# Weights' lower parts by ScalarE and an accumulating transfer, in one hybrid decoder layer in float32 on one core

## Chip, core and metric

One NeuronCore of a Trainium2 chip runs the whole layer as one program. The metric is the device time of one execution in microseconds (us). Engines: TensorE (PE), VectorE (DVE), ScalarE (ACT), GpSimd (POOL) and SyncE (SP), which here issues the transfers.

## What is computed

The input is x, 512 positions by 1024 channels in float32. In brief:

```python
proj = x @ w_in    # q, k, v of mixer A, q, k, v of mixer B, indexer q, k and weights, branch gates
# A: sparse attention, 12 heads of 64. Indexer scores of 8 heads choose 128 causal keys per query.
# B: dilated window attention, 12 heads in three groups, joined by their softmax denominators.
y = (sigmoid(gA) * (oA @ w_branch_a) + sigmoid(gB) * (oB @ w_branch_b)) @ w_out
x = LN(alpha * x + y)
x = LN(alpha * x + (silu(x @ w_ffn_gate) * (x @ w_ffn_up)) @ w_ffn_down)
```

All products are wanted to float32's accuracy.

## The kernel before

**Products of three.** TensorE multiplies in the type float32r, which keeps fewer bits. So each operand is split into an upper part hi, the value rounded to float32r, and a lower part lo, the value minus hi. A product is hi times hi, plus hi times lo, plus lo times hi: three matmuls of 128 x 128 weights with up to 512 columns.

**Units.** The weights lie in memory as units of 128 x 1024 (512 KB). `load_unit` (L354) takes one: a transfer from SP's queue into a buffer raw, a copy by ScalarE into whi (L363), and a subtraction raw minus whi into wlo (`sub`, L381) by an engine that the caller names. raw, whi and wlo have four buffers each. In the projections the callers name "POOL" (two subtractions of 128 x 512 on GpSimd) or, for the gates, "ANY" (GpSimd or VectorE). The first four units are loaded in four pieces together with x and are subtracted on VectorE or "ANY". From the branch products on (`load_unit("DVE")`, `halves`) VectorE subtracts.

**Tasks.** ORDER (L53) is a string of names that are carried out in that order. i0 to i3 project the indexer's queries, K its keys and weights, I0 to I3 are its scores, each T is four steps of the search for the 128 best keys. a0 to a11 project mixer A's queries and keys, W0 to W2 its values, H0 to H5 are pairs of its heads. d0 to d3, e0 to e7 and v project mixer B's queries, keys and values, B0 to B3 are its scores (`scores` L631, `pair_scores` L623), X the exchange of its softmax statistics, M0 to M3 its outputs. G0 to G15 are the gates. A projection of queries or keys does not come in the shape that the scores need: its rows are brought into place by moves, transfers from SBUF to SBUF that SP issues (`move`, and `put_s`; all SP transfers have line L347).

**The keys' chain.** `index_keys` takes three units (K), copies the keys (L696), turns them on VectorE (L706, L709, L710), has TensorE transpose them (L715), and splits the result (L718, L719). Only then the scores of I can start.

**The exchange.** `exchange` writes the statistics z1 and z23 to memory (d) and reads them back in the other order (z1r, z23n). `b_factors` (L867 to L876) makes factors of them, with which L891 (VectorE) and L892 (ScalarE) scale the probabilities; TensorE then transposes those (L787, in `b_mix`).

**What sets the order.** `Plan` records all operations with a cost in us and a lag, and `Plan.order` lays them out: whenever an engine is free it takes the ready operation that was recorded first. Costs and lags are the kernel's own numbers. The result is written out as each engine's instruction stream, and the engines keep to it: an engine that waits for one instruction does none of those behind it. In the plan GpSimd's operations and VectorE's "shared" ones exclude each other (TURNS).

Of the kernel before, what the change touches and what calls it, by code (L numbers as in the profile page):

```python
# [9 lines left out]
FT = mybir.dt.float32  # L10
# [39 lines left out]

ORDER = ("G10 i0 G12 G6 G2 e0 i1 i2 K e1 I1 d0 i3 I2 I3 G7 G1 d1 e4 I0 W0 d2 e2 B0 T T T T W2 e3 a8 B1 d3 T v G3 T "  # L53
         "e5 a0 T T e6 B2 T e7 B3 X W1 a1 G9 M1 a9 M0 a2 T G5 M3 M2 a3 a4 T a10 T T H1 G14 H0 a5 G8 a6 H4 H2 G15 "
         "a11 a7 H5 G13 H3 G11 G4 G0").split()

H = (slice(0, 64), slice(64, 128))
SWAP = [x ^ 8 for x in range(32)]
# [42 lines left out]
class Plan:  # L101
# [2 lines left out]

    LAT = {"PE": 0.2, "DVE": 0.16, "ACT": 0.17, "POOL": 0.12, "SP": 0.05}
    TO_PE = 0.22
    TURNS = {"DVE": "POOL", "POOL": "DVE"}
    SAME = {"PE": 0.0, "DVE": 0.13, "ACT": 0.155, "POOL": 0.1, "SP": 0.0}  # L110

    def __init__(self):
        self.ops, self.tags, self.groups, self.pools = [], {}, {}, {}
# [192 lines left out]
def layer(ctx, tc, xT, xN, pos, wp, bg, ln, cst, out):  # L306
# [2 lines left out]
    V, A, G = nc.vector, nc.scalar, nc.gpsimd  # L309

    pool = lambda name, bufs, **k: ctx.enter_context(tc.tile_pool(name=name, bufs=bufs, **k))
    NS = 82
    P.group("s", NS, pool("s", NS), "s")
    P.group("raw", 4, pool("raw", 4), "raw")
    P.group("whi", 4, pool("whi", 4), "whi")
# [37 lines left out]
    def load_unit(lo_eng, pieces=1):  # L353

        u = unit[0]
        unit[0] += 1
        raw, hi, lo = P.buf("raw", FT, (128, 1024)), P.buf("whi", FR, (128, 1024)), P.buf("wlo", FR, (128, 1024))
        n = 1024 // pieces

        def piece(i):  # L360
            c = slice(i * n, (i + 1) * n)
            dma(raw, lambda: raw[:, c], lambda: wp[u * 128:(u + 1) * 128, c], 512 * n, key=i)
            P.op("ACT", ac(n, 1), lambda e: A.activation(hi[:, c], raw[:, c], AF.Copy), [(raw, i)], [(hi, i)])  # L363
            m = n if lo_eng == "DVE" else min(n, 512)
            for j in range(n // m):
                x = slice(i * n + j * m, i * n + j * m + m)
                sub(lo_eng, m, lambda x=x: lo[:, x], lambda x=x: raw[:, x], lambda x=x: hi[:, x].bitcast(FT),
                    [(raw, i), (hi, i)], [(lo, (i * n + j * m) * KO // 1024)])
        if pieces == 1:
            piece(0)  # L370
        return hi, lo, pieces, piece
# [46 lines left out]
    def next_unit(lo_eng):  # L418
        return first_units.pop(0) if first_units else load_unit(lo_eng)
# [168 lines left out]

    def sides(name, j, puts, regroup=False, t0=0):

        p = project(next_unit("POOL"), t0=t0)
        if j == 0:
            turned[name] = rotated_parts(p, regroup, t0)
            return
        parts = plain_parts(p, regroup, t0)
        for s, put in enumerate(puts):
            for unit_, row, n, first in plain_rows(s):
                if unit_ == j - 1:
                    if first == 0:
                        put(turned[name], ROT * s, ROT, 0)  # L600
                    put(parts, row, n, ROT + first)
# [58 lines left out]

    def value_chunk():
        res = []
        natural([next_unit("POOL") for _ in range(2)], 4, 256, lambda b, p: res.append(value_tile(p)))
        return res

    def strided_values():


        ps = [P.buf("pv") for _ in range(NB)]
        for u in range(4):  # L670
            hi, lo = next_unit("POOL")[:2]
            for k in range(2):
                for b, p in enumerate(ps):
                    def f(e, hi=hi, lo=lo, k=k, ko=2 * u + k, b=b, p=p):
                        t = lambda x: nat(x.tile)[:, :, b]
                        w = slice(k * 512, k * 512 + 512)
                        nc.tensor.matmul(p.tile, t(xhi[ko]), hi[:, w], start=ko == 0, stop=False)
                        nc.tensor.matmul(p.tile, t(xlo[ko]), hi[:, w], start=False, stop=False)
                        nc.tensor.matmul(p.tile, t(xhi[ko]), lo[:, w], start=False, stop=ko == KO - 1)
                    P.op("PE", 3 * mm(512), f, [hi, lo, xhi[2 * u + k], xlo[2 * u + k]], [p])  # L680
        store["V0"], store["V1"] = [], []
        for p in ps:
            for i in range(2):
                store[f"V{i}"].append(value_tile(p, 256 * i))
# [4 lines left out]
    def index_keys():  # L689

        store["VB"] = []
        wi = fixed("wi", (128, NB, 8))
        kn = P.buf("rt", FT, (128, NB, 2, 64))

        def use(b, p):
            P.op("ACT", ac(128), lambda e: A.activation(  # L696
                kn[:, b], p[:, None, 256:320].to_broadcast([128, 2, 64]), AF.Copy), [p], [(kn, b), (p, 1)])
            store["VB"].append(value_tile(p))
            P.op("DVE", 0.075, lambda e: V.tensor_scalar(wi[:, b, :], p[:, 320:328], IDX_SCALE, None, ALU.mult),
                 [p], [(wi, b)])  # L700
        natural([next_unit("POOL") for _ in range(3)], 3, 328, use)
        t = P.buf("rt", FT, (128, 2, NB, 2, 2, 8))
        x = lambda h: kn[:, :, :, h * 8:h * 8 + 8]
        for i, m in enumerate((cn_rows, sn_rows)):
            for h in range(2):
                P.op("DVE", dv(64), lambda e, i=i, m=m, h=h: V.tensor_tensor(  # L706
                    t[:, i, :, :, h, :], x(h), m()[:, :, None, :].to_broadcast([128, NB, 2, 8]), ALU.mult),
                    [kn, cn, sn], [(t, (i, h))])
        P.op("DVE", dv(64), lambda e: V.tensor_sub(x(0), t[:, 0, :, :, 0, :], t[:, 1, :, :, 1, :]), [t], [kn])  # L709
        P.op("DVE", dv(64), lambda e: V.tensor_add(x(1), t[:, 0, :, :, 1, :], t[:, 1, :, :, 0, :]), [t], [kn])  # L710
        pk = P.buf("tp")

        def f(_):
            for b in range(NB):
                nc.tensor.transpose(pk[:, b * 128:(b + 1) * 128], kn[:, b].rearrange("p a d -> p (a d)"), ident())  # L715
        P.op("PE", 4 * 0.109, f, [kn, (cs, 1)], [pk])
        kh, kl = P.buf("qk", FR), P.buf("qk", FR)
        P.op("ACT", ac(512), lambda e: A.activation(kh.tile, pk.tile, AF.Copy), [pk], [kh])  # L718
        P.op("DVE", dv(512), lambda e: V.tensor_sub(kl.tile, pk.tile, kh.tile.bitcast(FT)), [pk, kh], [kl])  # L719
        for b in range(1, NB):  # L720
            a = P.buf("acc", FT, (128, (b + 1) * 128))
            P.op("POOL", 0.4, lambda e, a=a, b=b: G.memset(a[:, :b * 128], 0.0), [], [(a, 0)])
            P.op("POOL", 0.4, lambda e, a=a, b=b: G.tensor_copy(a[:, b * 128:], cs[:, C_G1 + 128:C_G1 + 256]),
                 [(cs, 1)], [(a, 1)])
            acc[b] = a
        idx.update(kh=kh, kl=kl, wi=wi)
# [259 lines left out]
    gates = {}  # L986

    def gate(j):
        p = project(next_unit("ANY"))
        t = P.buf("g")  # L990
        P.op("ACT", ac(512, 1), lambda e: A.activation(
            t.tile, p.tile, AF.Identity, bias=bgt[:, j:j + 1]), [p, bgt], [t])
# [339 lines left out]
```

## Time and profile before

| | us |
|---|---|
| median of three runs | 866.59 (865.05 to 868.48) |
| the profiled execution | 863.42 |
| its span, first to last instruction | 861.6 |
| TensorE busy | 844.8 |
| VectorE busy | 478.6 |
| ScalarE busy | 351.0 |
| GpSimd busy | 139.8 |

Projections and attention fill the span up to about 390 us, the branch products and w_out follow up to about 500 us, then the feed-forward part. "Busy" counts the time in which at least one instruction of an engine runs; TensorE's are pipelined, so a busy TensorE isn't one at its peak rate. The waits of an engine are the idle times before its instructions, put down to the semaphore that came last. The granted clock is TensorE's, 1.00 being 2.4 GHz. A row with xN merges N instructions that follow each other. A transfer's "us to landing" runs from its issue to the semaphore that tells of its end.

### The profile page before, as it was taken

The page shows a single profiled execution, that of the slowest core. Times are in us where ns is not written, and L with a number is a line of the kernel's source. Part 1 is how long each engine was busy: PE and PEld are TensorE (multiplying, and loading weights), DVE is VectorE, ACT ScalarE, POOL GpSimd, SP SyncE. Part 2 cuts the span into 40 slices and gives each one's busy share as a digit, 9 for nine tenths or more (in the row PEclk, how much of TensorE's full clock was granted, in tenths as well). Part 3 has the DMA queues.
Part 4 walks back from the last instruction along what each step waited for, and adds up shares of the span by engine and source line. Part 5 has one row for each costly group of instructions (what it writes and reads, how often), then busy time and mean ns, then how long its engine had stood idle before and what let it go on. Part 6 is the DMA issues. An engine that isn't in the chain of part 4 may idle for free.

```text
span 861.6 us, 11775 instructions
## 1 busy us (share of the span) xinstructions
PE 844.8 (98%) x4183; PEld 719.2 (83%) x4183; DVE 478.6 (56%) x1092; ACT 351.0 (41%) x752; POOL 139.8 (16%) x127
## 2 busy tenths in 40 slices
PE   8998899999999999999999999999999999999996
PEld 6897799898988888887888898888888888888885
DVE  6427379995477885796886543333333333222337
ACT  6433444433665596798740132222222222212300
POOL 1543433634233313110000000000000000000001
PEclk9999999999999999999999999999999999999999
DMA  6543444643353544323672022222222222222302
GB/s 214 185 157 94 141 146 117 188 134 112 82 184 98 166 139 143 115 84 99 207 263 91 1 74 98 98 94 93 95 93 95 97 96 98 98 98 99 98 24 74
DMA packets 46331, 100.82 MB, mean 117 GB/s; under 512 B 10304, under 2 KB 17728, under 8 KB 46272
## 3 DMA queue, kind: packets, MB, share of 16 engines
q1 hardware_dynamic: 46272, 100.07, 36.4%
q8 instruction: 33, 0.54, 0.2%
q14 instruction: 26, 0.21, 0.1%
HBM read 79.55 MB, written 2.13 MB: 95 GB/s over the span
## 4 chain that ended last, share of the span: by engine, by line
PE 89%; DVE 4%; SPq 2%; ACT 2%; DMA 2%; issue 1%; DVEq 0%; ACTq 0%
PE ps L1150 9%; PE ps L1149 9%; PE ps L1151 9%; PE ps L430 7%; PE ps L429 7%; PE ps L431 7%; PE ps L1178 5%; PE ps L1176 5%; PE ps L1177 5%; PE ps L631 2%; SPq L347 2%; PE ps L787 2%; PE ps L1116 2%; PE ps L1115 2%; PE ps L1042 2%; PE ps L1041 2%
## 5 line engine op out<-in xcount | busy, mean ns | idle before, releaser
L363 ACT ACTIVATE whi<-raw 128x1024 fp32r<-128x1024 f32 (+1 forms) x138 | 135.4, 985 | 181.8 <-issue 80.1
L381 DVE TENSOR_TENSOR wlo<-raw,whi 128x1024 fp32r<-128x1024 f32 (+2 forms) x99 | 101.7, 1029 | 155.9 <-ACT whi L363 155.8
L381 POOL TENSOR_TENSOR wlo<-raw,whi 128x512 fp32r<-128x512 f32 x92 | 121.7, 1346 | 219.5 <-ACT whi L363 178.6
L429 PE MATMUL ps<-s,whi 128*128 128x512 f32 (+1 forms) x352 | 140.1, 398 | 0.9 <-ACT whi L363 0.9
L1149 PE MATMUL ps<-s,whi 128*128 128x512 f32 (+1 forms) x368 | 139.8, 380 | 0.0
L1150 PE MATMUL ps<-s,whi 128*128 128x512 f32 (+1 forms) x368 | 139.8, 380 | 0.0
L1151 PE MATMUL ps<-s,wlo 128*128 128x512 f32 (+1 forms) x368 | 139.8, 380 | 0.0
L430 PE MATMUL ps<-s,whi 128*128 128x512 f32 (+1 forms) x352 | 136.6, 388 | 0.4 <-DVE s L381 0.4
L431 PE MATMUL ps<-s,wlo 128*128 128x512 f32 (+1 forms) x352 | 136.4, 387 | 0.0
L1089 POOL TENSOR_TENSOR z<-z,nhalf 128x1 f32<-128x1 f32 x8 | 7.6, 956 | 479.3 <-DVE z L1088 479.3
L1149 PEld LDWEIGHTS ps<-s,whi 128*128 128x128 f32 x368 | 69.2, 188 | 13.2
L1151 PEld LDWEIGHTS ps<-s,wlo 128*128 128x128 f32 x368 | 69.2, 188 | 13.2
L1150 PEld LDWEIGHTS ps<-s,whi 128*128 128x128 f32 x368 | 69.2, 188 | 12.9
L431 PEld LDWEIGHTS ps<-s,wlo 128*128 128x128 f32 x352 | 66.2, 188 | 13.2 <-DVE wlo L381 0.2
L430 PEld LDWEIGHTS ps<-s,whi 128*128 128x128 f32 x352 | 66.6, 189 | 11.9 <-DVE s L381 2.3
L429 PEld LDWEIGHTS ps<-s,whi 128*128 128x128 f32 x352 | 66.6, 189 | 11.6 <-ACT whi L363 1.3
L1176 PE MATMUL ps<-whi,s 128*128 128x512 f32 x136 | 52.9, 389 | 0.0
L1177 PE MATMUL ps<-wlo,s 128*128 128x512 f32 x136 | 52.9, 389 | 0.0
L1178 PE MATMUL ps<-whi,s 128*128 128x512 f32 x136 | 52.9, 389 | 0.0
L1163 ACT ACTIVATE s<-ps 128x512 f32<-128x512 f32 x22 | 13.2, 598 | 86.8 <-PE ps L1151 86.8
L1164 DVE TENSOR_TENSOR s<-s,ps 128x512 f32<-128x512 f32 x22 | 15.1, 687 | 55.4 <-PE ps L1151 55.3
L808 DVE TENSOR_TENSOR s<-ps,s 128x128 fp32r<-128x128 f32 (+1 forms) x144 | 39.1, 316 | 9.9 <-ACT s L806 9.1
(167 smaller groups left out, 1460.9 us busy)
## 6 DMA issues: line engine op xcount, KB each, us to landing
raw<-in_wp SPq DMA_DIRECT2D x135, 512.0 KB, 3.4
s<-s SPq DMA_DIRECT2D x88, 96.0 KB, 2.3
s<-s SPq DMA_DIRECT2D x136, 32.0 KB, 2.0
raw<-in_wp SPq DMA_DIRECT2D x16, 128.0 KB, 4.2
s<-in_xT SPq DMA_DIRECT2D x8, 256.0 KB, 4.5
s<-in_ln SPq DMA_DIRECT2D x8, 256.0 KB, 5.5
s<-in_xN SPq DMA_DIRECT2D x8, 256.0 KB, 5.6
out<-s SPq DMA_DIRECT2D x7, 256.0 KB, 2.0
```

Of the source, the lines that this page charges most:

```text
L363: P.op("ACT", ac(n, 1), lambda e: A.activation(hi[:, c], raw[:, c], AF.Copy), [(raw, i)], [(hi, i)])
L381: P.op(eng, cost, lambda e: ENG[e].tensor_tensor(dst(), a(), b(), ALU.subtract), reads, writes, shared=True)
L429: nc.tensor.matmul(p[:, t0:], hi[:, c], xhi[ko][:, t0:], start=ko == 0, stop=False)
L430: nc.tensor.matmul(p[:, t0:], hi[:, c], xlo[ko][:, t0:], start=False, stop=False)
L431: nc.tensor.matmul(p[:, t0:], lo[:, c], xhi[ko][:, t0:], start=False, stop=ko == KO - 1)
L808: subs.append((dv(m), lambda e, src=src, dst=dst, hi=hi, ho=ho, lo=lo, lo_o=lo_o: V.tensor_tensor(dst(lo, lo_o), src(), dst(hi, ho).bitcas ...
L1149: nc.tensor.matmul(p[:, c], hi[:, k], x1hi[ko][:, c], start=ko == 0, stop=False)
L1150: nc.tensor.matmul(p[:, c], hi[:, k], x1lo[ko][:, c], start=False, stop=False)
L1151: nc.tensor.matmul(p[:, c], lo[:, k], x1hi[ko][:, c], start=False, stop=ko == KO - 1)
L1176: nc.tensor.matmul(sums[:, :cols], hs[k][0][:, t], hi(), start=k == first, stop=False)
L1177: nc.tensor.matmul(sums[:, :cols], hs[k][0][:, t], lo(), start=False, stop=False)
L1178: nc.tensor.matmul(sums[:, :cols], hs[k][1][:, t], hi(), start=False, stop=k == last)
```

## The change

For 53 units (all of the projections but the first four) `load_unit` gets lo_eng "DMA". ScalarE then writes minus the upper part into wlo, a second pass over 128 x 1024 that reads whi. A transfer issued by GpSimd adds the unit's weights from memory to it in place (accum_op add), so that wlo ends as weights minus upper part. GpSimd's 92 subtractions and 14 of VectorE are gone. In the plan the issue is an operation of an engine "PQ" of its own, with a cost of 1.1 and a lag of 3.5; in the program it stands in GpSimd's stream. The pool s has 80 buffers instead of 82, the descriptor area is 4096 instead of 512 bytes. ORDER is another one, and the weights are packed in its order. The matmuls are the same 4183, in another order.

```diff
-ORDER = ("G10 i0 G12 G6 G2 e0 i1 i2 K e1 I1 d0 i3 I2 I3 G7 G1 d1 e4 I0 W0 d2 e2 B0 T T T T W2 e3 a8 B1 d3 T v G3 T "
+ORDER = ("G10 i0 G12 G6 i1 d0 e0 i2 i3 e1 K I1 I0 I3 I2 G7 e4 T T T e2 e3 G5 T a4 G9 d1 d2 T T a0 B0 B1 e5 v d3 T "
...
-    LAT = {"PE": 0.2, "DVE": 0.16, "ACT": 0.17, "POOL": 0.12, "SP": 0.05}
+    LAT = {"PE": 0.2, "DVE": 0.16, "ACT": 0.17, "POOL": 0.12, "SP": 0.05, "PQ": 0.1}
...
-    NS = 82
+    NS = 80
...
+            if lo_eng == "DMA":
+
+                P.op("ACT", ac(n, 1), lambda e: A.activation(lo[:, c], hi[:, c].bitcast(FT), AF.Copy, scale=-1.0),
+                     [(hi, i)], [(lo, i)])
+                P.op("PQ", 1.1, lambda e: G.dma_start(lo[:, c], wp[u * 128:(u + 1) * 128, c],
+                                                      accum_op=ALU.add), [(lo, i)], [(lo, i)], lag=3.5)
+                return
...
-        p = project(next_unit("POOL"), t0=t0)
+        p = project(next_unit("DMA"), t0=t0)
...
-        p = project(next_unit("ANY"))
+        p = project(next_unit("DMA"))
...
-    nc = _bacc.Bacc("TRN2", target_bir_lowering=False, num_devices=1, dynamic_dma_scratch_size=512)
+    nc = _bacc.Bacc("TRN2", target_bir_lowering=False, num_devices=1, dynamic_dma_scratch_size=4096)
```

The same replacement stands in `value_chunk`, `strided_values` and `index_keys`. Line numbers behind L363 are 7 higher in the changed kernel (L368 is the new transfer, L366 the new copy).

Behind the first four units, on ScalarE. Before (ps_188 and ps_201 are the sums of the last two of the four units; L991 adds a gate's bias, L526 splits a turned projection):

```order
L363 ACTIVATE whi_386<-raw_320 128x1024
L363 ACTIVATE whi_394<-raw_336 128x1024
L991 ACTIVATE s_404<-ps_188,bgt 128x512
L363 ACTIVATE whi_408<-raw_347 128x1024
L526 ACTIVATE s_420<-s_388 128x384
L991 ACTIVATE s_435<-ps_201,bgt 128x512
L363 ACTIVATE whi_441<-raw_354 128x1024
```

Now, at the same place (wlo_414 is the lower part of the fifth unit):

```order
L363 ACTIVATE whi_386<-raw_320 128x1024
L363 ACTIVATE whi_394<-raw_336 128x1024
L998 ACTIVATE s_405<-ps_188,bgt 128x512
L533 ACTIVATE s_409<-s_388 128x384
L366 ACTIVATE wlo_414<-whi_386 128x1024
L366 ACTIVATE wlo_424<-whi_394 128x1024
L998 ACTIVATE s_432<-ps_201,bgt 128x512
L363 ACTIVATE whi_436<-raw_347 128x1024
L363 ACTIVATE whi_440<-raw_354 128x1024
```

The fifth unit's negated copy stands behind both upper parts, a bias and a split; GpSimd issues its transfer right after it, and TensorE's order has the fifth unit directly behind the first four.

At the keys' transposes, on TensorE. Before (ps_711 is the last of K's four sums, ps_747 a gate's unit, L715 the transposes):

```order
L646 MATMUL ps_711<-wlo_574,s_318 128x328
L429 MATMUL ps_747<-s_148,whi_610 128x512
L430 MATMUL ps_747<-s_155,whi_610 128x512
L431 MATMUL ps_747<-s_148,wlo_622 128x512
L429 MATMUL ps_747<-s_186,whi_610 128x512
L430 MATMUL ps_747<-s_198,whi_610 128x512
L431 MATMUL ps_747<-s_186,wlo_622 128x512
L429 MATMUL ps_747<-s_205,whi_610 128x512
L430 MATMUL ps_747<-s_224,whi_610 128x512
L431 MATMUL ps_747<-s_205,wlo_622 128x512
L715 MATMUL ps_776<-cs,s_644 128x128 x4
```

Now (ps_869 is a gate's unit, L722 the transposes; the first product of ps_869, directly behind K's last, is the row ahead of these):

```order
L437 MATMUL ps_869<-s_155,whi_724 128x512
L438 MATMUL ps_869<-s_148,wlo_736 128x512
L436 MATMUL ps_869<-s_186,whi_724 128x512
L437 MATMUL ps_869<-s_198,whi_724 128x512
L438 MATMUL ps_869<-s_186,wlo_736 128x512
L436 MATMUL ps_869<-s_205,whi_724 128x512
L437 MATMUL ps_869<-s_224,whi_724 128x512
L438 MATMUL ps_869<-s_205,wlo_736 128x512
L436 MATMUL ps_869<-s_227,whi_724 128x512
L437 MATMUL ps_869<-s_265,whi_724 128x512
L438 MATMUL ps_869<-s_227,wlo_736 128x512
L722 MATMUL ps_904<-cs,s_758 128x128 x4
```

Twelve products of 512 columns stand behind K's last sum instead of nine.

At the exchange, on SP. Before (d_95 and d_96 are z1 and z23 in memory, the s rows are moves, the raw rows loads of units):

```order
L347 DMA z1r<-d_95 128x32
L347 DMA s_2570<-s_2354 16x512
L347 DMA s_2600<-s_2364 16x512 x2
L347 DMA s_2619<-s_2354 16x512
L347 DMA d_96<-z_92 128x32
L347 DMA s_2619<-s_2364 16x512
L347 DMA raw_2652<-in_wp 128x1024
L347 DMA raw_2668<-in_wp 128x1024
L347 DMA z23n<-d_96 128x4x8
```

Now:

```order
L347 DMA d_95<-z_91 128x4x8
L347 DMA raw_2315<-in_wp 128x1024
L347 DMA raw_2327<-in_wp 128x1024
L347 DMA z1r<-d_95 128x32
L347 DMA s_2346<-s_1719 16x512
L347 DMA s_2346<-s_1797 16x512
L347 DMA s_2365<-s_1719 16x512 x2
L347 DMA d_96<-z_92 128x32
L347 DMA s_2384<-s_1797 16x512 x2
L347 DMA s_2403<-s_1719 16x512
L347 DMA z23n<-d_96 128x4x8
```

Four moves stand between z1r and the write of d_96 in either order; two loads of units moved from between d_96 and z23n to ahead of z1r. On TensorE 36 products of 512 columns and 12 of 256 stand between the last pair scores, whose statistics d_96 takes, and the first transposes (L794); in the old order 48 of 512 and 27 of 256 stood there.

## Rows read from the trace of the kernel before

**Rows 1.** The page, busy us (share of the span) and instructions by engine.

```profile
PE 844.8 (98%) x4183; PEld 719.2 (83%) x4183; DVE 478.6 (56%) x1092; ACT 351.0 (41%) x752; POOL 139.8 (16%) x127
```

**Rows 2.** TensorE's waits up to 400 us: total us, times, longest us.

```profile
PE ps L715 <- DVE s L710: 2.6, 1, 2.6
...
PE ps L631 <- DMA s<-s: 2.3, 1, 2.3
...
PE ps L818 <- ACT s L806: 0.4, 1, 0.4
```

**Rows 3.** Busy us by stretch: PE, PEld, DVE, ACT, POOL, granted clock, DMA share, GB/s.

```profile
20.00:380.00 360.00, 354.14 (x1942) 312.18 (x1941) 248.33 (x712) 193.01 (x487) 130.13 (x110) 1.00 0.45 136
...
60.00:80.00 20.00, 17.40 (x91) 14.93 (x90) 12.69 (x24) 9.22 (x17) 6.86 (x8) 1.00 0.26 80
...
80.00:100.00 20.00, 17.70 (x82) 15.22 (x81) 9.20 (x13) 7.96 (x15) 8.96 (x8) 0.91 0.51 157
...
300.00:380.00 80.00, 80.00 (x448) 68.59 (x447) 60.49 (x248) 63.84 (x216) 17.43 (x13) 1.00 0.43 128
...
540.00:560.00 20.00, 20.00 (x90) 16.55 (x89) 6.11 (x7) 4.69 (x7) 0.00 (x0) 1.00 0.30 104
```

**Rows 4.** The page's groups of instructions: GpSimd's subtractions (busy us, mean ns | idle before).

```profile
L381 POOL TENSOR_TENSOR wlo<-raw,whi 128x512 fp32r<-128x512 f32 x92 | 121.7, 1346 | 219.5 <-ACT whi L363 178.6
```

**Rows 5.** Timeline around the keys' transposes: start us, us, engine, line [wait].

```profile
63.62 3.75 POOL L381 TENSOR_TENSOR wlo<-raw,whi 128x512 fp32r<-128x512 f32 x3
...
63.91 3.68 DVE L706 TENSOR_TENSOR s<-s,s 128x64 f32<-128x64 f32 x4
...
68.12 0.63 PE L715 MATMUL ps<-cs,s 128*128 128x128 f32 x4 [2.60 <-DVE s L710]
```

**Rows 6.** Line L706: ns of one, least/median/most.

```profile
L706 DVE TENSOR_TENSOR s<-s,s x4: 210/1193/1309, 63.9 to 67.4; 128x64 f32<-128x64 f32 x4
```

**Rows 7.** Chain of waits ahead of the index scores: start us, us, what.

```profile
87.59 5.00 DMA s<-s
```

**Rows 8.** Timeline of ScalarE behind the first four units.

```profile
25.25 2.02 ACT L363 ACTIVATE whi<-raw 128x1024 fp32r<-128x1024 f32 x2
...
28.67 0.54 ACT L526 ACTIVATE s<-s 128x384 fp32r<-128x384 f32 x1
```

**Rows 9.** Timeline of TensorE at the fifth unit.

```profile
29.72 0.39 PE L429 MATMUL ps<-s,whi 128*128 128x512 f32 x1
...
30.18 0.39 PE L431 MATMUL ps<-s,wlo 128*128 128x512 f32 x1
```

**Rows 10.** Transfers: KB each, median us from issue to landing.

```profile
raw<-in_wp SPq DMA_DIRECT2D x135, 512.0 KB, 3.4
...
z1r<-d SPq DMA_DIRECT2D x1, 16.0 KB, 2.7
...
z23n<-d SPq DMA_DIRECT2D x1, 16.0 KB, 4.4
```

**Rows 11.** Timelines of ScalarE, SP, VectorE and TensorE at the exchange.

```profile
236.42 0.19 ACT L836 ACTIVATION_READ_ACCUMULATOR s<-s,z 128x1 f32 x1
...
238.47 0.53 SPq L347 DMA_DIRECT2D d<-z  x1
...
240.73 0.38 SPq L347 DMA_DIRECT2D z23n<-d  x1
...
245.26 0.16 DVE L867 TENSOR_TENSOR f<-z,z23n 128x16 f32<-128x16 f32 x1
...
247.50 0.69 DVE L381 TENSOR_TENSOR wlo<-raw,whi 128x512 fp32r<-128x512 f32 x1
...
249.08 0.18 DVE L876 TENSOR_TENSOR f<-f,f 128x16 f32<-128x16 f32 x1
...
249.75 0.55 PE L787 MATMUL ps<-cs,s 128*128 128x128 f32 x3 [0.24 <-ACT s L892]
```

**Rows 12.** SP's transfers (L347), all of them.

```profile
DMA to landing us min/median/max: 1.6/2.6/7.4
```

More of the change, by code (lines that the diff above doesn't have):

```diff
@@ L47 @@
 NCONST = C_H + 8
-ORDER = ("G10 i0 G12 G6 G2 e0 i1 i2 K e1 I1 d0 i3 I2 I3 G7 G1 d1 e4 I0 W0 d2 e2 B0 T T T T W2 e3 a8 B1 d3 T v G3 T "
-         "e5 a0 T T e6 B2 T e7 B3 X W1 a1 G9 M1 a9 M0 a2 T G5 M3 M2 a3 a4 T a10 T T H1 G14 H0 a5 G8 a6 H4 H2 G15 "
-         "a11 a7 H5 G13 H3 G11 G4 G0").split()
+ORDER = ("G10 i0 G12 G6 i1 d0 e0 i2 i3 e1 K I1 I0 I3 I2 G7 e4 T T T e2 e3 G5 T a4 G9 d1 d2 T T a0 B0 B1 e5 v d3 T "
+         "a8 e6 G1 B2 e7 B3 T T G13 X G8 M0 T a1 W0 a9 M2 M1 T a2 G0 W1 M3 a10 T T W2 H0 a11 H4 a3 H1 G2 a5 a6 H5 "
+         "a7 H2 G11 G3 H3 G4 G15 G14").split()
 H = (slice(0, 64), slice(64, 128))
@@ L101 @@
 class Plan:
-    LAT = {"PE": 0.2, "DVE": 0.16, "ACT": 0.17, "POOL": 0.12, "SP": 0.05}
+    LAT = {"PE": 0.2, "DVE": 0.16, "ACT": 0.17, "POOL": 0.12, "SP": 0.05, "PQ": 0.1}
     TO_PE = 0.22
     TURNS = {"DVE": "POOL", "POOL": "DVE"}
-    SAME = {"PE": 0.0, "DVE": 0.13, "ACT": 0.155, "POOL": 0.1, "SP": 0.0}
+    SAME = {"PE": 0.0, "DVE": 0.13, "ACT": 0.155, "POOL": 0.1, "SP": 0.0, "PQ": 0.0}
     def __init__(self):
@@ L662, in value_chunk @@
         res = []
-        natural([next_unit("POOL") for _ in range(2)], 4, 256, lambda b, p: res.append(value_tile(p)))
+        natural([next_unit("DMA") for _ in range(2)], 4, 256, lambda b, p: res.append(value_tile(p)))
         return res
@@ L670, in strided_values @@
         for u in range(4):
-            hi, lo = next_unit("POOL")[:2]
+            hi, lo = next_unit("DMA")[:2]
             for k in range(2):
@@ L700, in use @@
                  [p], [(wi, b)])
-        natural([next_unit("POOL") for _ in range(3)], 3, 328, use)
+        natural([next_unit("DMA") for _ in range(3)], 3, 328, use)
         t = P.buf("rt", FT, (128, 2, NB, 2, 2, 8))
```

## The prediction

> **What bounds the kernel now.** I read the page's busy times first, then TensorE's waits, then the busy times by stretch, and last the timelines around each wait.
>
> TensorE is busy 844.8 us of a span of 861.6 us [rows 1], so all that any change off TensorE can win is its idle time. The waits of TensorE up to 400 us are few: 2.6 us for VectorE at the transposes of the index keys (L715), 2.3 us for a move at the index scores (L631), and small change [rows 2]. In the table by stretch both fall between 60 and 100 us, where TensorE loses 2.6 and 2.3 us of 20, and the second stretch has a granted clock of 0.91 while the mean from 20 to 380 us is 1.00 [rows 3]. There it stepped from 2.4 to 1.2 GHz behind the wait, which costs 0.09 of 20 us, 1.8 us. From 20 to 380 us the DMA engines are busy 0.45 of the time and ScalarE 193 of 360 us; in the heads' stage, 300 to 380 us, ScalarE has 63.8 of 80 us [rows 3].
>
> The profiled execution took 863.42 us, 3.2 us under the median of the runs, 866.59 us. I work out differences against that execution and put them on the median. 0.5% is 4.3 us, about what a measurement of this kernel can tell from no change.
>
> **The change part by part.**
>
> *GpSimd's subtractions go.* 92 half units at 1346 ns [rows 4], 122 us, leave an engine that TensorE does not wait for, so by themselves they are worth nothing. What they cost is seen on VectorE: the four small products of L706 take 3.68 us beside a run of three subtractions that began on GpSimd at 63.62 us, and the transposes behind them start at 68.12 us after 2.60 us of waiting [rows 5]. The quickest of the four took 210 ns, the middle 1193 ns [rows 6]: at 210 ns all four need 0.8 us. The new order also puts 12 products ahead of these transposes instead of 9. On the other side ScalarE has one more pass of 1.0 us near there. I take -2.6 us, with -1.5 as the other end. 7 units' subtractions leave VectorE too (14 halves); nothing on TensorE waits for those, so 0.
>
> *The index units move forward.* The 2.3 us wait at L631 was for a move that took 5.00 us to land [rows 7] behind a queue of moves; only 27 products of 512 columns, 6 us at 0.23 us each, stood between unit i3 and its scores. Now 66 such products and 96 of 328 columns stand there, 15 + 14 us. The wait goes, and with it the clock's step: -2.3 and -1.8, together -4.1 us; the other end is -1, if the queue of moves grows by as much.
>
> *53 passes on ScalarE, 53 transfers.* A pass over 128x1024 takes 1.0 us (two in 2.02 us [rows 8]), so ScalarE gets 53 us more. In straight projections a unit occupies TensorE for 24 x 0.227 = 5.4 us (of the products that start at 29.72 and 30.18 us the second is two behind the first [rows 9]), and with four buffers a lower part has about three units, 16 us, from the release of its buffer to its use. Against that stand two passes, 2 us, and the transfer. For the transfer there is no row: it reads the same 512 KB from the same rows as a raw load, which lands 3.4 us after issue [rows 10], and must read the destination as well. The lower end is 3.4 us. A second read of 512 KB is 1.6 us: in the feed-forward stretch 104 GB/s of plain loads keep the engines busy 0.30 of the time [rows 3], so 350 GB/s at full. I take 3.4 + 1.6 = 5.0 us, and 6.8, twice the load, as the upper end. In steady projections all three hide.
>
> *They do not hide at the first such unit.* ScalarE's order, shown with the change, and its times tell why: the two upper parts run from 25.25 to 27.27 us [rows 8]; behind them stand a gate's bias and L533, short passes of some 0.5 us (L526, today's L533, takes 0.54 us [rows 8]), and only then the first negated copy, from about 28.25 to 29.25 us; the transfer can start at 29.4 us. TensorE ends the first four units at 29.72 us, and its third product, at 30.18 us today, needs the lower part [rows 9]. Nothing else stands in its order, so it waits: 29.4 + 5.0 - 30.2 = **+4.2 us**, ends +2.6 and +6.0. Should the clock step down behind it as it did at 92 us, 1.8 us come on top; behind the 2.60 us wait at 68 us it did not (1.00 from 60 to 80 us [rows 3]), so I leave it for the upper end. The Trainium skill (DMA: Bandwidth & Descriptors, Anatomy of one DMA) fits a transfer issued from GpSimd with 2.0 us plus the bytes at 436 GB/s, 3.2 us here, an estimate that counts no second read; by it the wait would be 2.4 us and the sum 1.8 us lower. The rows give 3.4 us at the least.
>
> *The exchange comes with less cover.* Today 14 us of products stand between the last pair scores and the first transposes of b_mix, and TensorE still waits 0.2 us at their end [rows 11]. The chain: the last exponential ends at 236.61 us, d is issued at 238.47 us behind four moves, z23n at 240.73 us; it takes 4.4 us to land [rows 10], the factors run from 245.26 to 249.26 us, and the transposes follow at 249.75 us [rows 11]. The new order has 36 products of 512 and 12 of 256 columns there, 8.2 + 1.4 = 9.6 us. What shortens the chain: d need not wait for the four moves ahead of it (in the new order SP has reached them before the scores end, their sources being older), about 1.8 us, and the two halves of a lower part that VectorE computes among the factors, 0.6 us and more each ([rows 11] have one), 1.3 us, are gone; 14.5 - 3.1 = 11.4 us, and 9.7 us if z23n lands as z1r does, in 2.7 us [rows 10]. So TensorE waits 0.1 to 1.8 us; I take 1.1, **+0.9 us** net, -0.2 as one end and +3 as the other if both hops land as slowly as the 5.00 us row.
>
> *Heads' stage.* After H0 eleven units are still to be prepared, 11 us more on ScalarE, less seven scalings (19 of the heads' stand on ScalarE in the old order, 12 in the new), 3 us if each is near the 0.54 us above. ScalarE goes from 0.80 of the stage to about 0.88 (8 us more over some 100). TensorE is busy all 80 us of it today [rows 3]. I take **+1.0 us**, ends 0 and +4. The other first uses of moves keep 7.7 us or more of products ahead of them (today the shortest were 6.4 and 7.1): **+0.3 us**, ends -0.5 and +2.5.
>
> Two buffers fewer in the pool s, and the larger descriptor area, cost no time by themselves. From the branch products on nothing changes.
>
> Sum: -2.6 - 4.1 + 4.2 + 0.9 + 1.0 + 0.3 = **-0.3 us**: 863.1 us for the profiled execution, **866.3 us** for the median.
>
> **The rivals.**
>
> *Faster: the new waits stay at their lower ends.* -2.6 - 4.1 + 2.6 (the first unit), -0.2 (the exchange), 0 (ScalarE), -0.5 (first uses) and -0.4 for today's wait at L818 [rows 2] make -5.2: **861.4 us**. For it: all covers but one are longer than 7 us, and VectorE is no longer stretched. Against it: it needs the transfer to be as quick as a plain load.
>
> *Slower: transfers and moves get in each other's way.* 53 transfers of 1.6 to 3.2 us of all sixteen engines add 85 to 170 us to 162 us (0.45 of 360 us), a share of 0.69 to 0.92. A move lands in 2.6 us in the middle and 7.4 us at most today [rows 12]. If moves land 1.5 to 2.5 us later, the first unit waits 6.0 us and the clock falls, +1.8; the exchange has two hops, +3; three first uses with 7.7 to 8.4 us ahead come 1.5 us late each, +4.5; with ScalarE's +1.0 and the gains of -6.7 that is +9.6: **876.2 us**. It decides from where the added transfer takes more than about 6 us. For it: 5.00 us [rows 7] at a share of 0.51 [rows 3]. Against it: most covers are two or three units long. The Trainium skill (DMA: Bandwidth & Descriptors, Issuing engines are not separate DMA queues) says that transfers of all issuing engines run on the same sixteen engines and interleave, which is this rival's mechanism; the rows show one issuing engine only, so they cannot bear it out.
>
> *Slower: ScalarE becomes the bound of the heads' stage.* Its load grows by 11 - 3 = 8 us there, and if TensorE waits for most of it, 7.5 us instead of 1.0, the result is +6.2: **872.8 us**. It decides where ScalarE's in-order passes stand ahead of the exponentials; against it speak the 12% that stay free.
>
> **How the numbers follow.** No change to speak of: 0.43, own range 862.3 to 870.9 us (the two bounds of 0.5%). Faster: 0.29. Transfers in the way: 0.17. ScalarE: 0.11; both slower cases together 0.28. The range has to reach into both sides: from 858 us, under which I put 0.06, to 876.5 us, over which lies half of the rival with the transfers, 0.09.
>
> **What would show it.** Right: no wait at L722 over 0.5 us, none at L638 between 70 and 100 us, a granted clock of 1.00 there; one wait of 3 to 5 us of TensorE near 30 us for a transfer into wlo; a share of DMA of 0.65 to 0.8 from 20 to 380 us. Wrong: transfers that land 7 us or more after issue, TensorE waits for wlo at many units, or ScalarE over 0.95 from 300 to 380 us with waits of TensorE for it.

## The result, and the profile after

The changed kernel takes 895.65 us (median of four runs, 892.73 to 900.59) against 865.82 us before (864.74 to 868.48) in the same comparison: ratio 1.035, 95% interval 1.0304 to 1.0396. It is some 30 us slower, and the time is above the predicted range. The profiled execution took 895.8 us, its span is 894.0 us.

The page of the changed kernel, busy times, and its DMA queues (packets, MB, share of sixteen engines' span; q0 is the queue of GpSimd's transfers):

```profile
PE 854.9 (96%) x4183; PEld 728.3 (81%) x4183; DVE 459.3 (51%) x1089; ACT 401.9 (45%) x794; POOL 64.8 (7%) x88
...
q1 hardware_dynamic: 46272, 100.07, 35.2%
q0 software_dynamic: 7632, 27.79, 17.6%
```

Against [rows 1] GpSimd lost 75 us (its 122 us of subtractions went, 46 us of issues came) and ScalarE gained 51. The new queue holds all sixteen engines 0.176 x 894.0 / 53 = 2.97 us for each transfer. By stretch, the answer to [rows 3]:

```profile
20.00:380.00 360.00, 330.95 (x1757) 292.04 (x1755) 202.92 (x597) 214.01 (x436) 51.50 (x67) 0.96 0.82 196
60.00:80.00 20.00, 19.54 (x117) 18.30 (x116) 3.16 (x8) 7.54 (x13) 2.59 (x3) 1.00 0.81 168
80.00:100.00 20.00, 15.88 (x73) 13.14 (x72) 6.59 (x17) 12.59 (x20) 5.45 (x8) 0.91 0.93 249
300.00:380.00 80.00, 77.02 (x473) 68.29 (x472) 47.50 (x177) 57.02 (x157) 7.81 (x9) 0.98 0.73 180
```

The DMA share from 20 to 380 us went from 0.45 to 0.82, the granted clock from 1.00 to 0.96. TensorE's waits of 0.5 us and more, against [rows 2] (L630 and L638 are the scores, L438 a unit's product with its lower part, L722 the keys' transposes, L794 the transposes behind the exchange):

```profile
PE ps L630 <- DMA s<-s: 7.6, 2, 4.5
PE ps L438 <- DMA wlo<-in_wp: 6.3, 1, 6.3
PE ps L638 <- DMA s<-s: 5.2, 2, 3.1
PE ps L638 <- issue: 3.0, 1, 3.0
PE ps L794 <- DVE s L898: 2.3, 1, 2.3
PE ps L722 <- ACT s L663: 1.9, 1, 1.9
PE ps L638 <- ACT s L725: 1.8, 1, 1.8
PE ps L402 <- DVE s L398: 1.5, 1, 1.5
...
PE ps L653 <- DMA wlo<-in_wp: 0.5, 1, 0.5
```

All of TensorE's waits together are 31.4 us; before they were 9.3. These 22 us are two thirds of the 32.4 us by which the span grew. The rest is mostly products at 1.2 GHz behind such a wait: the mean granted clock of the span went from 0.996 to 0.983. Moves carry half of the waits, 7.6 + 5.2 + 3.0 = 15.8 us; before it was 3.0 us, 2.3 at L631 [rows 2] and 0.7 at L623. The 3.0 us that stand as "issue" are counted with them because they end 1.05 us after a move of 5.55 us has landed. The new transfers themselves carry one wait that counts. Issues of transfers (KB each, median us to landing), against [rows 10]:

```profile
raw<-in_wp SPq DMA_DIRECT2D x135, 512.0 KB, 3.7
wlo<-in_wp POOLq DMA_DIRECT2D x53, 512.0 KB, 6.2
s<-s SPq DMA_DIRECT2D x88, 96.0 KB, 4.0
s<-s SPq DMA_DIRECT2D x136, 32.0 KB, 3.4
```

The moves before:

```profile
s<-s SPq DMA_DIRECT2D x88, 96.0 KB, 2.3
s<-s SPq DMA_DIRECT2D x136, 32.0 KB, 2.0
```

Over all of SP's transfers the median and the longest landing rose, against [rows 12]:

```profile
DMA to landing us min/median/max: 1.8/3.9/10.7
```

Three places show how lateness reaches TensorE. At the fifth unit, the timelines of ScalarE, GpSimd and TensorE:

```profile
27.33 2.02 ACT L366 ACTIVATE wlo<-whi 128x1024 fp32r<-128x1024 f32 x2
...
28.72 1.93 POOL L368 DMA_DIRECT2D wlo<-in_wp  x2 [8.54 <-ACT wlo L366]
...
35.76 0.69 PE L438 MATMUL ps<-s,wlo 128*128 128x384 f32 x1 [6.33 <-DMA wlo<-in_wp]
```

The first transfer is issued at 28.72 us and takes 7.0 us to land, with the sixth unit's beside it; from 36 to 41 us the granted clock is 0.51, the lower of the two levels, which costs 2.4 us more. At the index scores, ScalarE's timeline and, in the last row, TensorE's:

```profile
84.20 1.06 ACT L363 ACTIVATE whi<-raw 128x1024 fp32r<-128x1024 f32 x1 [2.41 <-DMA raw<-in_wp]
...
89.62 1.06 ACT L363 ACTIVATE whi<-raw 128x1024 fp32r<-128x1024 f32 x1 [2.98 <-DMA raw<-in_wp]
90.58 0.58 ACT L725 ACTIVATE s<-ps 128x512 fp32r<-128x512 f32 x1
...
91.21 0.38 PE L638 MATMUL ps<-s,s 128*128 128x256 f32 x1 [1.83 <-ACT s L725]
```

ScalarE stood at the copy of a late load while the keys' copy, L725, was queued behind it. And the chain of waits ahead of two later groups of scores (start us, us, what):

```profile
150.12 7.25 DMA s<-s
157.37 0.97 PE ps L638 x3
...
208.27 9.74 DMA raw<-in_wp
...
218.65 2.06 DMA s<-s
220.72 1.60 PE ps L630 x6
```

One is behind a move of 7.25 us, the other behind a load of 9.74 us after which SP issued the next move.

### The profile page after: what moved, and what is told of

It is laid out like the page before. It is cut to its first block, busy times and chain, and to the rows that moved or that the text cites. A ratio compares the mean times of both kernels' runs of the same rounds, so it can differ in the third digit from the quotient of the medians.

```text
span 894.0 us, 11803 instructions
## 1 busy us (share of the span) xinstructions
PE 854.9 (96%) x4183; PEld 728.3 (81%) x4183; DVE 459.3 (51%) x1089; ACT 401.9 (45%) x794; POOL 64.8 (7%) x88
## 3 DMA queue, kind: packets, MB, share of 16 engines
q1 hardware_dynamic: 46272, 100.07, 35.2%
## 4 chain that ended last, share of the span: by engine, by line
PE 77%; DMA 10%; DVE 4%; SPq 4%; issue 2%; ACT 2%; DVEq 0%; ACTq 0%; POOLq 0%
PE ps L1158 9%; PE ps L1156 9%; PE ps L1157 9%; PE ps L438 5%; PE ps L436 5%; PE ps L437 5%; PE ps L1185 4%; PE ps L1184 4%; PE ps L1183 4%; SPq L347 4%; DMA raw<-in_wp 4%; PE ps L638 3%; DMA s<-s 3%; PE ps L794 2%; PE ps L1124 2%
## 5 line engine op out<-in xcount | busy, mean ns | idle before, releaser
L363 ACT ACTIVATE whi<-raw 128x1024 fp32r<-128x1024 f32 (+1 forms) x138 | 135.2, 985 | 188.7 <-issue 83.7
L388 DVE TENSOR_TENSOR wlo<-raw,whi 128x1024 fp32r<-128x1024 f32 (+1 forms) x85 | 91.2, 1073 | 154.3 <-ACT whi L363 154.1
L438 PE MATMUL ps<-s,wlo 128*128 128x512 f32 (+1 forms) x352 | 138.5, 393 | 6.3 <-DMA wlo<-in_wp 6.3
L438 PEld LDWEIGHTS ps<-s,wlo 128*128 128x128 f32 x352 | 67.7, 192 | 19.9 <-DMA wlo<-in_wp 6.6
L1157 PEld LDWEIGHTS ps<-s,whi 128*128 128x128 f32 x368 | 69.2, 188 | 13.2
L1156 PEld LDWEIGHTS ps<-s,whi 128*128 128x128 f32 x368 | 69.2, 188 | 12.9
L437 PEld LDWEIGHTS ps<-s,whi 128*128 128x128 f32 x352 | 68.1, 194 | 11.2 <-DVE s L388 1.4
L436 PEld LDWEIGHTS ps<-s,whi 128*128 128x128 f32 x352 | 68.3, 194 | 10.7 <-ACT s L412 1.0
L368 POOL DMA_DIRECT2D wlo<-in_wp x53 | 46.2, 873 | 332.5 <-ACT wlo L366 207.1
L366 ACT ACTIVATE wlo<-whi 128x1024 fp32r<-128x1024 f32 x53 | 56.3, 1067 | 0.9
L638 PE MATMUL ps<-s,s 128*128 128x256 f32 (+3 forms) x176 | 39.8, 342 | 10.4 <-DMA s<-s 5.2
```

The source lines that it names most:

```text
L388: P.op(eng, cost, lambda e: ENG[e].tensor_tensor(dst(), a(), b(), ALU.subtract), reads, writes, shared=True)
L436: nc.tensor.matmul(p[:, t0:], hi[:, c], xhi[ko][:, t0:], start=ko == 0, stop=False)
L437: nc.tensor.matmul(p[:, t0:], hi[:, c], xlo[ko][:, t0:], start=False, stop=False)
L438: nc.tensor.matmul(p[:, t0:], lo[:, c], xhi[ko][:, t0:], start=False, stop=ko == KO - 1)
L638: nc.tensor.matmul(p[:, :w], qs[:, t:t + 128], k[:, k0:k0 + w], start=n == 0, stop=n == 1)
L1156: nc.tensor.matmul(p[:, c], hi[:, k], x1hi[ko][:, c], start=ko == 0, stop=False)
```

## The experiments

Ratios are to the kernel before, measured in the same comparison. "Over the floor" is the time of a stretch less what its products take one behind the other at 2.4 GHz, by the spacing of undisturbed ones: 11.8 us from 20 to 380 us before, 44.8 after. Theory A is that the accumulating transfers crowd the DMA engines, so that moves and loads land late. Theory B is that the new order has too little cover, which means too few products between a transfer's start and its first use. Theory C is that ScalarE's added passes hold up what stands behind them.

**1. The parts apart.** The kernel before with the change's ORDER (e1); the change with the old ORDER (e2):

```diff
-ORDER = ("G10 i0 G12 G6 G2 e0 i1 ...
+ORDER = ("G10 i0 G12 G6 i1 d0 e0 ...
```

> The kernel before with the new ORDER alone: GpSimd and VectorE subtract as before, no added transfers, no added passes on ScalarE. Theory A (the added transfers crowd the sixteen DMA engines, so that moves and loads land late): the moves land in about 2.0 to 2.6 us as before, the share of DMA from 20 to 380 us stays near 0.45, and the time is within 1% of before, 860 to 874 us. Theory B (the new order itself leaves too few products ahead of the first uses of moves): most of the 30 us are here already, 885 us or more, with waits of TensorE for moves at the pair scores and the heads' scores.

> The changed kernel with the old ORDER: transfers, passes and pool sizes of the change, the order list of before. Theory A: the share of DMA rises to about 0.8 as in the changed kernel, the moves land in 3.4 to 4 us, and the time is 885 to 905 us. Theory B: with the old order's longer covers the transfers are hidden, 862 to 875 us.

e1: 859.74 us, ratio 0.9946 (0.9925 to 0.9966). e2: 905.55 us, ratio 1.0469 (1.0434 to 1.0504). The order is a gain, of 6 us without the transfers and 10 with them, and B falls. In e1 no wait for a move is over 0.5 us. Its stretch, and its longest wait:

```profile
20.00:380.00 360.00, 356.88 (x1961) 314.86 (x1960) 249.22 (x727) 198.19 (x499) 135.89 (x113) 1.00 0.45 137
```

```profile
PE ps L715 <- DVE s L710: 2.2, 1, 2.2
```

**2. The transfer weakened.** The accumulating transfer made a plain one (e3), cut to 128 of 1024 columns (e4) and to 512 (e5); the columns left out stay minus the upper part. Shortened:

```diff
-    G.dma_start(lo[:, c], wp[u * 128:(u + 1) * 128, c], accum_op=ALU.add)
+    G.dma_start(lo[:, c], wp[u * 128:(u + 1) * 128, c])                          # e3
+    G.dma_start(lo[:, :128], wp[u * 128:(u + 1) * 128, :128], accum_op=ALU.add)  # e4; :512 in e5
```

> The changed kernel with plain transfers in place of the accumulating ones: the same instructions in the same order, but the destination isn't read back and the lower part is the weights themselves, so the subtraction is left out. Theory A: one such transfer takes about 1.6 us of the sixteen engines in place of 2.97, the share of DMA from 20 to 380 us falls from 0.82 to about 0.64, the waits for moves shrink to less than half: 874 to 884 us. Theory B: the waits stay, 890 us or more. If it is the issue from GpSimd as such (its queue, not the bytes), the time also stays at 890 us or more.

> The changed kernel with accumulating transfers of the first 128 of 1024 columns only: same instructions, same order, an eighth of the added bytes; seven eighths of each lower part are left at minus the upper part. Theory A: the share of DMA falls to about 0.5, moves land in 2.0 to 2.6 us, the time is 862 to 872 us, with the wait at the fifth unit down from 6.3 us to 2 to 3 us. Theory B: nothing but the fifth unit's wait changes, 885 us or more. A third theory, C (ScalarE's 53 added passes hold up what stands behind them): the passes are all still there, so 880 us or more, with waits of TensorE for ScalarE.

> The change with each of the 53 accumulating transfers cut to 512 of 1024 columns (256 KB); the other half of each lower part stays minus the upper part. The change's order, ScalarE's passes and all waits stay. So far: no transfer 859.7 us (share of the DMA engines 0.45 in 20:380), 128 columns 860.6 (0.53), 1024 columns 895.6 (0.82). Theory A1 (capacity with a knee: nothing is lost until the engines are crowded): share near 0.62 to 0.66, moves land in at most 2.8 us, 860 to 868 us. Theory A2 (cost in proportion to the bytes): (895.6 - 860.6) x 3/7 + 860.6 = 875.6 us, 872 to 880. Theory D (the number of transfers or of descriptors, not the bytes, is what costs): as 128 columns, 859 to 862.

e3: 867.84 us, ratio 1.0029 (1.001 to 1.0048), under the 874 to 884 us that theory A had asked for. e4: 860.58 us, 0.9952 (0.9937 to 0.9967). e5: 867.4 us, 1.002 (1.001 to 1.0029). e4 keeps the order, all of ScalarE's passes and all 53 issues, and is as fast as e1: C falls as the cause of the 36 us, and so does a cost by the number of transfers. The same stretch as above, in e4 (with its longest wait), e5 and e3:

```profile
20.00:380.00 360.00, 355.91 (x1949) 314.60 (x1949) 232.15 (x717) 244.55 (x535) 53.73 (x69) 0.99 0.53 145
```

```profile
PE ps L438 <- ACT wlo L366: 3.5, 1, 3.5
```

```profile
20.00:380.00 360.00, 350.56 (x1916) 309.26 (x1915) 226.08 (x696) 239.17 (x520) 54.02 (x69) 0.99 0.68 173
```

```profile
20.00:380.00 360.00, 350.99 (x1920) 309.98 (x1918) 226.95 (x699) 239.63 (x523) 37.20 (x71) 0.99 0.70 212
```

At shares of 0.45, 0.53, 0.68, 0.70 and 0.82 the times are 859.7, 860.6, 867.4, 867.8 and 895.7 us: nothing, then 8 us, then 36. Not the kind of transfer but the share of the engines sorts these: half an accumulating transfer and a whole plain one come out alike, while the bytes a second differ (173 and 212 GB/s). The costs are not in proportion, which had asked for 872 to 880 us from e5.

The "nothing" of e4 is a balance of two places. At the fifth unit e4 waits 3.5 us, which the profile puts down to ScalarE's copies, and from 20 to 40 us it is 6.6 us over the floor, where e1 has 0.1. At the keys' transposes e1 waits 2.2 us and from 60 to 80 us is 5.3 us over the floor, where e4 has 0.2. e5 and e3 have the same two differences from e1, 6.2 and 6.3 us from 20 to 40 us and nothing from 60 to 80. In the rest of 20 to 380 us e1, e4, e5, e3 and the change are 3.2, 4.3, 11.3, 10.4 and 35.2 us over the floor, and that is the same bend.

**3. Is it the second read?** raw, in SBUF, as the source (e7); raw is then held until the transfer has read it.

```diff
-    G.dma_start(lo[:, c], wp[u * 128:(u + 1) * 128, c], accum_op=ALU.add)
+    G.dma_start(lo[:, c], raw[:, c], accum_op=ALU.add)
```

> The change with raw, which is in SBUF already, as the source of the accumulating transfers instead of the weights in memory. Same result; raw's four buffers are held until the transfer ends. Theory M (the second read from memory is the cost: HBM or its path): landing falls from 6.2 to 4.5 us or less, the queue's time below 2.2 us of all sixteen engines each, 862 to 875 us. Theory N (the adding itself, element by element on the DMA engines, is the cost): time of the engines 2.7 to 3.1 us each as before, share 0.80 to 0.84, 890 to 905 us, raw's longer hold adds some.

915.06 us, ratio 1.0553 (1.0522 to 1.0584), above the 890 to 905 us of theory N. The transfers' queue in e7 and in e3:

```profile
q0 software_dynamic: 7632, 27.79, 16.5%
```

```profile
q0 software_dynamic: 7632, 27.79, 10.6%
```

With spans of 915.6 and 866.0 us these are 2.85 and 1.73 us of all sixteen engines a transfer, against the change's 2.97. Reading the weights from memory again isn't the cost; that the transfer adds is, 1.7 times a plain transfer of the same bytes (whether by the adding itself or by reading the destination for it was not separated). That e7 is slower than the change agrees with raw's longer hold; this was not separated.

**4. Whose lateness?** Each transfer in two: 128 columns that the products wait for, and 896 into a scrap buffer that nobody reads (e9).

```diff
+                x = scrap[u % 2]
...
+                    G.dma_start(lo[:, :128], wp[u * 128:(u + 1) * 128, :128], accum_op=ALU.add)
+                    return G.dma_start(x[:, 128:], wp[u * 128:(u + 1) * 128, 128:], accum_op=ALU.add)
```

> The change with each accumulating transfer in two: 128 columns to the lower part, which the products wait for, and the other 896 columns of the same weights to a scrap buffer that nobody reads (two of them in turn; the pool s has 76 instead of 80 buffers). The other columns of the lower part stay minus the upper part. The DMA engines do about what they do in the change, the products wait for 64 KB alone. Narrow transfers alone gave 860.6 us (share 0.53), the change 895.6 (0.82). Theory P (crowding: the transfers make the moves and loads of others late): share 0.78 to 0.84, moves land in 3.2 us or more, waits at L630 and L638 come back, 880 to 897 us. Theory Q (what counts is that products wait for their own long transfer): moves' lateness stays covered, 860 to 870 us.

894.58 us, ratio 1.035 (1.0334 to 1.0366), the same as the change, where e4, whose products wait for the same 64 KB, took 860.58. The stretch, and TensorE's longest waits (lines are 7 higher than in the change):

```profile
20.00:380.00 360.00, 333.89 (x1772) 293.02 (x1772) 206.38 (x610) 217.24 (x445) 96.74 (x119) 0.96 0.84 198
```

```profile
PE ps L729 <- ACT s L670: 9.1, 1, 9.1
PE ps L801 <- DVE s L905: 4.4, 1, 4.4
PE ps L801 <- DVE s L790: 3.6, 5, 0.9
PE ps L445 <- DMA wlo<-in_wp: 3.1, 1, 3.1
```

Only 3.1 of 29.1 us of waits are for a lower part, and even that transfer (64 KB) took 5.4 us in the middle, where it took 3.0 in e4. The waits stand in other places than in the change (moves 5.0 us instead of 15.8, both with "issue"; the keys' transposes, L729, 9.1 behind a load of 6.56 us), but the sum is nearly the same as the change's 31.4. It is work that nobody waits for, on the engines, that costs the time. GpSimd also issues twice as many transfers there and is busy 97 of 360 us; no wait of TensorE names it, but whether it adds to the time was not separated.

**5. The fifth unit alone** subtracted by VectorE (e10).

```diff
+            if lo_eng == "DMA" and u == 4:
+                lo_eng = "DVE"
```

> The change with the fifth unit alone subtracted by VectorE instead of ScalarE and a transfer; same result. In the change TensorE waits 6.3 us there and runs about 5 us at 1.2 GHz behind it, together some 8.7 us over the floor in 20:40. If this wait is a loss of its own: 895.6 - 8 = 887.6 us, 885 to 890. If work behind it only takes the time over (next transfer late instead): 892 to 896. The later waits (L630, L638, L722) are not expected to change by more than 2 us in sum.

893.32 us, ratio 1.033 (1.0307 to 1.0353). The wait of 6.3 us at the fifth unit went (0.7 us left at L440), and about 2 of its 8 us came out at the end. The later waits changed by more than expected: two waits for wlo at the keys' units (L655) are 5.7 us, where the change had 0.5. All waits together are 29.5 us. Which wait a late transfer ends in is a matter of place; the sum hardly moves.

**6. A plan that knows** (lags of 5.5 for the transfers, 3.0 for moves, 0.5 more for loads; e8), and **every other unit** (e6; odd units on GpSimd).

```diff
-    lag=3.5
+    lag=5.5
-    lag=1.75 if reads else 2.1 + nbytes / 500e3
+    lag=3.0 if reads else 2.6 + nbytes / 500e3
```

> The change with a plan that knows what the trace of the change shows: lag of the accumulating transfer 5.5 instead of 3.5, of moves 3.0 instead of 1.75, of loads 0.5 more. ORDER, transfers and passes stay; the instruction streams are laid out anew. Theory F (the plan's lags were too short; the engines' capacity is enough): most of the waits at L630, L638 and L438 go, 862 to 872 us. Theory A (capacity: the engines are crowded in 20:380 whatever the order): share stays 0.80 to 0.84, waits move elsewhere, 885 to 900 us.

> The change with the accumulating transfer for every other unit only; the others are subtracted on GpSimd as before. Same result, the change's order. The bytes of the transfers are those of the half-width kernel, in half as many transfers of full size. Theory A1 (crowding with a knee): 860 to 868 us, share 0.62 to 0.66. Theory A2 (in proportion): 873 to 880. Theory E (a single transfer's landing of 6 us on the path is what costs, wherever one stands): units that are taken from raw to product in a hurry still wait, about half of the loss is left, with the fifth unit's wait only if the fifth is one of those that are transferred.

e8: 891.28 us, ratio 1.0295 (1.028 to 1.031), share 0.81: better by some 5 us, not by 25. e6: 876.26 us, ratio 1.0119 (1.0102 to 1.0135), share 0.64: halfway in bytes, but 9 us over e5, which has the same bytes in twice as many transfers. Of its waits 5.4 us are the fifth unit's for wlo, 3.2 us for d and 2.6 us at the keys' transposes for the keys that VectorE turns. GpSimd's subtractions are back as well, so e6 doesn't tell whether the size of a transfer counts besides the share; that stays open. Nor does the share alone sort all runs: e6 at 0.64 is slower than e3 at 0.70, and e7, with 915 us at 0.78, than the change at 0.82.

**7. One queue or sixteen engines?** The 53 units' loads from ScalarE's queue (e13).

```diff
+            if lo_eng == "DMA":
+                P.op("ACT", 0.2, lambda e: A.dma_start(raw[:, c], wp[u * 128:(u + 1) * 128, c]),
+                     [], [(raw, i)], lag=2.1 + 512 * n / 500e3)
+            else:
...
```

> The change with the 53 units' weights loaded from ScalarE's queue instead of SP's; moves and all else stay on SP's queue. Same result, same bytes. Theory R (one queue: a move lands late because it stands behind 512 KB loads on SP's own queue, and SP's issue is held): moves back to 2.6 us or less, no wait for issue, 865 to 882 us. Theory A (the sixteen engines are shared by whatever is in flight, on any queue): moves land in 3.2 us or more, share 0.80 to 0.84, 885 to 905 us; ScalarE's issues may hold it, which adds some.

890.51 us, ratio 1.0282 (1.0261 to 1.0303), share 0.82. Its issues:

```profile
raw<-in_wp SPq DMA_DIRECT2D x82, 512.0 KB, 3.2
raw<-in_wp ACTq DMA_DIRECT2D x53, 512.0 KB, 6.0
wlo<-in_wp POOLq DMA_DIRECT2D x53, 512.0 KB, 7.6
s<-s SPq DMA_DIRECT2D x88, 96.0 KB, 4.2
s<-s SPq DMA_DIRECT2D x136, 32.0 KB, 3.3
```

Moves land as late with the loads on a queue of their own, so it isn't SP's queue that makes them late. What makes the 5 us to the change is not shown. By the Trainium skill (DMA: Bandwidth & Descriptors, Issuing engines are not separate DMA queues) transfers of all issuing engines run on the same sixteen engines and interleave. With three issuing engines, and moves at 4.2 and 3.3 us against 4.0 and 3.4, these rows agree.

**8. Without the DMA engines.** e1 with VectorE doing all 53 units' subtractions (e11), e1 with a true lag of moves (e12), and e11 with GpSimd for the fifth unit alone (e14). The first replacement stands in the four other places too.

```diff
-        p = project(next_unit("POOL"), t0=t0)
+        p = project(next_unit("DVE"), t0=t0)
...
+        if u == 4:
+            lo_eng = "POOL"
```

> The kernel before with the change's order, and VectorE instead of GpSimd for the subtractions of all 53 units. Same result, no accumulating transfer, no added ScalarE pass. VectorE gets 92 subtractions of 0.69 us, some 63 us, in 20:380, where it is busy 206 of 360 us now; GpSimd's 124 us go. With the order alone 859.7 us. If VectorE's slack is enough: 856 to 861 us, share of the DMA engines 0.45. If VectorE's queue becomes the wait (masks' search, splits behind subtractions): 862 to 875 us with waits of TensorE for VectorE.

> The kernel before with the change's order, and 2.3 instead of 1.75 as the moves' lag in the plan (they land in 2.0 to 2.3 us by the trace). Same result. With the order alone 859.7 us, whose waits for moves are 0.3 us at most in one place: if nothing is left to gain there, 858 to 861 us; a gain over 1 us would show that its 1.2 GHz stretches at 74 to 80 us go; a loss up to 3 us if the new layout opens another wait.

> The kernel before with the change's order, VectorE subtracting 52 of the 53 units and GpSimd the fifth, where the kernel with VectorE alone waited 3.0 us and lost some 4.8 us more than the one with GpSimd alone (5.06 against 0.25 over the floor in 20:40). Same result. If that loss goes and nothing follows: 860.0 - 4.8 = 855.2 us, 854 to 857. If the next wait takes it over: 858 to 861. The order alone, with GpSimd: 859.7.

e11: 860.05 us, ratio 0.9939 (0.9916 to 0.9962), with a new wait of 3.0 us at the fifth unit. e12: 860.43 us, 0.9955 (0.9939 to 0.9972), no gain. e14: 856.48 us, ratio 0.9889 (0.9873 to 0.9906), the fastest of all, 9 us faster than the kernel before. Its stretch:

```profile
20.00:380.00 360.00, 358.05 (x1966) 316.51 (x1967) 288.49 (x768) 201.72 (x505) 10.74 (x18) 1.00 0.45 137
```

VectorE is busy 288 of 360 us and TensorE 358: VectorE had the room for what was given to the DMA engines. Five to six of the 9 us are the order's (e1, 0.9946). VectorE in place of GpSimd gains nothing over e1 in e11, and some 4 us more once the fifth unit's wait is gone (0.9889 against e11's 0.9939).

## Why the prediction was wrong

Its likeliest case was no change, 866.3 us. The step that failed is what the 53 transfers cost outside the fifth unit. "In steady projections all three hide" puts it at nothing, and "The other first uses of moves", +0.3 us, takes moves to land as before. The transfers did hide, with 0.5 us of waits for a lower part behind the fifth unit. But they made others late: the larger moves landed in 4.0 us in the middle instead of 2.3, and TensorE waited 15.8 us for moves instead of 3.0. The prediction priced what the new transfers wait for and who waits for them, and left out what they do to transfers of others. The case that came is the rival "transfers and moves get in each other's way", at a chance of 0.17 and 876.2 us. Its mechanism, that the transfers make moves late on engines they share, is what e3, e4, e5, e9 and e13 show: its engine time, 1.6 to 3.2 us, holds the 2.97 measured, its share of 0.69 to 0.92 the 0.82, and its turning point, a transfer over about 6 us, the 6.2. Its size was off by 20 us. It gave three first uses 1.5 us each, and had no price for ScalarE and SP, which keep their order and stand at a late load with others' work behind them. It counted the products at 1.2 GHz behind one new wait, not behind each. The trace of before had the warning, which the prediction names for this rival: a move of 5.00 us [rows 7] in a stretch whose DMA share was 0.51 [rows 3].

Point by point:

- *The transfer, 5.0 us (3.4 to 6.8).* 6.2 us in the middle, 5.2 at least and 10.3 at most, 7.0 at the place that counted. The price was a plain load's landing plus the engines' time for a second read (at the 350 GB/s that it reads off, 512 KB are 1.5 us, not the 1.6 of the sum); e7 shows that it isn't the read from memory. The Trainium skill (DMA: Bandwidth & Descriptors, Anatomy of one DMA) would make it 3.2 us, an estimate; the trace disagrees, and even the plain transfers of e3 took 5.1 us.
- *The fifth unit, +4.2 us.* The place, the engine order and the wait were as told; it took 6.3 us, and 2.4 for the clock. ScalarE was 0.9 us earlier than costed (the first copy starts at 27.33 us, expected at 28.25). e10 shows that as a term of a sum it was wrong: taken away, it gives back about 2 us.
- *Keys' transposes, -2.6 us.* The four products of VectorE took 0.22 us each without GpSimd beside them, against [rows 6], and in e2 (old order) and e4 there is no wait here, so the cause was read rightly. Quick products are not enough, though: in e1 they also take 0.22 us, but no product stands between K's last sum and the transposes, and the wait is 2.2 us. In the change 1.9 us came back through ScalarE, which waited 2.41 us for a load first.
- *Index units, -4.1 us.* The order alone did it: in e1 80 to 100 us has 0.2 us over the floor, where before has 4.1. In the change ScalarE's wait for a load took its place, and the clock is 0.91 as before [rows 3].
- *The exchange, +0.9 us.* 2.3 us at L794, and a clock of 0.91 from 240 to 260 us: d took 5.0 us and z1r 6.7 to land, the "both hops land slowly" end, against [rows 10].
- *Heads' stage, +1.0 us for ScalarE.* This did not come: no wait for ScalarE there, 57 of 80 us busy, 0.71 (the stage begins later; from 300 to 400 us it is 76.9 of 100). The 3 us that TensorE lost from 300 to 380 us are the wait that ends behind the move of 5.55 us named above.
- *Other first uses, +0.3 us.* 15.8 us at L630 and L638: the largest part of the miss.

Of what was to show it right, only the wait near 30 us for a lower part came, and longer: L722 waited 1.9 us, L638 1.8 us near 91 us with a clock of 0.91, and the share was 0.82, over the 0.65 to 0.8. Of what was to show it wrong, waits at many units did not come (two, at L438 and L653); some transfers did land 7 us or more after issue, but not the one in the middle (6.2 us).

## What to carry to other kernels

A transfer has two prices: when it lands, and how long it holds the DMA engines that all other transfers need. Sum the second over a stretch before moving arithmetic there: against the order alone this kernel lost 1 us at a share of 0.53, 8 us at about 0.7 and 36 us at 0.82, although 18% of the engines' time was still free. These figures are of one order of work and of transfers in like pieces (e6 lost some 16 us at 0.64), and a high share costs only where something waits for a late transfer: from 40 to 60 us the change's share was 0.94, and TensorE was busy all 20 us. Where short transfers feed the critical engine, look first for an engine with room of its own: VectorE, busy 249 of 360 us in e1, took the same work, and the kernel stayed as fast (e11) or became a little faster (e14).

## What the runs showed of the hardware

- An accumulating transfer of 512 KB (128 x 4 KB, float32) from GpSimd held the sixteen engines 2.97 us, a plain one 1.73 us (e3), and an accumulating one from SBUF 2.85 us (e7). GpSimd was busy 0.87 us to issue one.
- The same 512 KB load from ScalarE's queue landed in 6.0 us in the middle while GpSimd's transfers ran, and held the engines as long as from SP's queue: 9.5% of a span of 890.0 us is 1.60 us each, and SP's queue fell from 35.2% of 894.0 us to 25.7% of 890.0, 1.62 us for each of the 53 (e13).
- A move of 96 KB landed in 2.4 us in the middle at a share of 0.53 (e4), 2.9 at 0.68 (e5) and 4.0 at 0.82 (the change).
- Four VectorE products of 128 x 64 with both inputs in SBUF took 976 ns each in the mean while GpSimd subtracted beside them (before), and 218 ns without (the change).
